# Merge gates of a two-layer hybrid block: one plain projection over 1152 tokens, or plain products for 512 and Strassen's products for 640

## Chip, cores, metric

One core of a Trainium2 chip. The metric is device time of the whole program in microseconds (us). Before the change three runs took 2002.78, 2003.73 and 2006.33 us (median 2003.73).

## What is computed

Two layers over 1152 tokens (128 context, 1024 latent) of width 1024. In each layer h is the normalised, modulated input; `h @ w_in` gives the inputs of three branches (Fourier mixing, retention, windowed attention) and, in its last 3072 columns, the merge gates. At the end of a layer:

```python
ga, gb, gc = jnp.split(jax.nn.sigmoid(mg), N_BRANCH, axis=-1)
merged = ga * (ya @ w_pa) + gb * (yb @ w_pb) + gc * (yc @ w_pc)
out = merged @ w_out
x = x + gate * rms_norm(out, g_post)
```

`mg` is 1152 x 3072 with a contraction over 1024; ya and yb have 256 columns, yc (the attention's output) has 512.

## The kernel before

Tokens lie along the free axis: `HH` and `HL` hold h transposed, as a high part (a 32-bit type that TensorE multiplies in one pass, "f32r") and the low rest, 8 blocks of 128 rows by 1152 tokens each. Every projection multiplies in three terms: high weight by high h, high weight by low h, low weight by high h. A weight unit is 1024 x 128: SP loads it to `raw` (two buffers, 512 KB), ACT casts the high part (L174), POOL subtracts the low part (L175), both with three buffers.

The gates are made in `branch` (L923), once per branch `br` and block `j` of 128 output columns. For each of three chunks of 384 tokens `proj_t` (L214) puts 24 matmuls into a PSUM bank of tag `pj` (two banks), ACT takes the tanh (L957, sigmoid as 0.5 + 0.5 tanh), PE multiplies the branch's y by its projection (L960 to L962), and DVE forms (1 + tanh) times that (L963). Branch 0 stores the sum to DRAM (`scr_m0`), branch 1 loads it, adds its own on POOL (L975) and stores (`scr_m1`), branch 2 adds the last and keeps it in the tiles `M0` to `M7`. From these comes h for the output projection (L1207, L1208).

Branches 0 and 1 stand in the program behind the attention (L983 to L1176), whose chain is QK on PE (L1057), maxima on DVE (L1071, L1075), exp on ACT (L1094), transposes on PE (L1111), casts on ACT and DVE (L1114, L1115), PV on PE (L1117, L1118). A list scheduler of the framework, with a timeline of its own, sets one fixed order for each engine's queue, and puts the branches' matmuls between those of the attention. Each engine works through its queue in order and waits on semaphores. All DMAs are issued by SP, also in order. `tick` (L481) adds a step of the next modulation vector: one load and two DVE operations on 128x256 (L446).

## Time and profile before

| | |
|---|---|
| median of three runs | 2003.73 us |
| the profiled execution | 2000.78 us, span 1999.0 us |
| PE busy | 1947.7 us (97%) |
| DVE, ACT, POOL busy | 51%, 34%, 28% |
| DMA | 230.53 MB, 115 GB/s on average |

A matmul's busy time overlaps the next one's, so a share near 100% means that PE had something in flight, and the price of a matmul is the distance from its start to the next start. The layers lie at about 100 to 960 us and 960 to 1999 us; attention with its interleaved gates at about 400 to 790 and 1390 to 1770 us; branch 2 after it.

### The profile page before, as it was taken

The numbers are of one execution on the slowest core, as the hardware profiler recorded it, in microseconds if no ns is written. First come the engines' busy times: TensorE is split into PE (matmuls) and PEld (weight loads), VectorE is DVE, ScalarE is ACT, GpSimd is POOL, SyncE is SP. The second block draws the span as 40 slices with busy tenths as digits, with TensorE's granted clock in tenths as the row PEclk, the third lists the DMA queues.
The fourth block names the chain that finished last, engine by engine and source line by source line (L and its number), as shares of the span: only waits on it lengthen the run. The fifth ranks groups of instructions, "written<-read, shape, count | busy, mean of one in ns | idle before, by whom it ended". The sixth has DMA issues, their size and how long they took to land.

```text
span 1999.0 us, 29840 instructions
## 1 busy us (share of the span) xinstructions
PE 1947.7 (97%) x11022; PEld 1790.3 (90%) x11022; DVE 1010.4 (51%) x2575; ACT 676.5 (34%) x1535; POOL 550.4 (28%) x424
## 2 busy tenths in 40 slices
PE   5999899999999999999999999999999999999998
PEld 2898788999999999999878978899999999999987
DVE  6735657556677765104675262443555665410411
ACT  2522111235555444114331212022555554421411
POOL 2222232111122332434441214122121222333442
PEclk9999999999999999999999999999999999999999
DMA  8323554353333334223344235234422433422142
GB/s 292 106 72 98 137 156 136 112 177 99 103 119 113 117 107 146 80 89 128 116 142 98 63 96 163 73 118 135 116 87 84 120 103 95 145 90 83 59 154 85
DMA packets 245186, 230.53 MB, mean 115 GB/s; under 512 B 37920, under 2 KB 215856, under 8 KB 244784
## 3 DMA queue, kind: packets, MB, share of 16 engines
q1 hardware_dynamic: 245040, 228.62, 37.8%
q8 instruction: 87, 1.43, 0.3%
q14 instruction: 59, 0.48, 0.1%
HBM read 170.14 MB, written 58.42 MB: 114 GB/s over the span
## 4 chain that ended last, share of the span: by engine, by line
PE 84%; DMA 6%; DVE 5%; issue 2%; ACT 2%; POOL 1%; SPq 1%; DVEq 0%; POOLq 0%; ACTq 0%
PE pj L218 13%; PE pj L220 13%; PE pj L219 13%; PE pj L228 5%; PE pj L229 5%; PE pj L230 5%; PE tr L1111 3%; DMA raw<-in_w_in 2%; PE sl L1057 2%; PE pv L1118 2%; PE pv L1117 2%; PE sl L962 2%; PE pj L960 2%; PE sl L960 2%; PE pj L961 2%
## 5 line engine op out<-in xcount | busy, mean ns | idle before, releaser
L218 PE MATMUL pj<-HH,uh 128*128 128x384 f32 x1440 | 491.7, 341 | 9.0 <-DVE grz L237 2.9
L219 PE MATMUL pj<-HL,uh 128*128 128x384 f32 x1440 | 486.2, 338 | 0.0
L220 PE MATMUL pj<-HH,ul 128*128 128x384 f32 x1440 | 486.0, 337 | 0.0
L175 POOL TENSOR_TENSOR ul<-raw,uh 128x1024 fp32r<-128x1024 f32 x80 | 192.2, 2403 | 481.1 <-ACT uh L174 380.4
L218 PEld LDWEIGHTS pj<-HH,uh 128*128 128x128 f32 x1440 | 271.5, 189 | 14.3 <-ACT mth L957 4.9
L219 PEld LDWEIGHTS pj<-HL,uh 128*128 128x128 f32 x1440 | 271.7, 189 | 1.6
L220 PEld LDWEIGHTS pj<-HH,ul 128*128 128x128 f32 x1440 | 271.6, 189 | 1.5
L174 ACT CAST uh<-raw 128x1024 fp32r<-128x1024 f32 x80 | 83.9, 1049 | 179.3 <-PE pj L219 124.6
L446 DVE SCALAR_TENSOR_TENSOR macc<-mw,siluc,macc 128x256 f32<-128x256 f32 x224 | 135.3, 646 | 10.9 <-DMA mw<-in_w_mod 10.9
L228 PE MATMUL pj<-uh,HH 128*128 128x512 f32 x336 | 133.5, 398 | 3.9 <-ACT kv L546 1.8
L229 PE MATMUL pj<-ul,HH 128*128 128x512 f32 x336 | 132.6, 395 | 0.0
L230 PE MATMUL pj<-uh,HL 128*128 128x512 f32 x336 | 132.5, 394 | 0.0
L963 DVE SCALAR_TENSOR_TENSOR M<-M,sl 128x384 f32<-128x384 f32 x48 | 26.6, 554 | 201.8 <-PE sl L962 196.6
L1094 ACT ACTIVATE E<-E,NM 128x640 f32<-128x640 f32 (+1 forms) x128 | 101.9, 798 | 64.1 <-DVE NM L1090 63.9
L1115 DVE TENSOR_TENSOR El<-tr,Eh 128x512 fp32r<-128x512 f32 x132 | 88.9, 685 | 46.3 <-ACT Eh L1114 46.0
L1114 ACT CAST Eh<-tr 128x512 fp32r<-128x512 f32 x132 | 74.7, 587 | 88.8 <-PE tr L1111 87.1
L975 POOL TENSOR_TENSOR mth<-mth,ml 128x384 f32<-128x384 f32 x48 | 51.4, 1071 | 178.0 <-DVE mth L963 114.3
L963 DVE SCALAR_TENSOR_TENSOR mth<-mth,pj 128x384 f32<-128x384 f32 x96 | 52.9, 551 | 62.5 <-ACT mth L957 32.0
L1111 PE MATMUL tr<-ident,E 128*128 128x128 f32 x528 | 84.0, 272 | 0.2 <-ACT E L1094 0.2
L975 POOL TENSOR_TENSOR M<-M,mrow 128x384 f32<-128x384 f32 x48 | 48.6, 1015 | 124.9 <-DVE M L963 66.5
L1075 DVE CUSTOM_DVE_ANT_0 E<-sl,mask,m 128x384 f32<-128x384 f32 (+1 forms) x128 | 72.1, 578 | 17.4 <-PE sl L1057 17.0
L228 PEld LDWEIGHTS pj<-uh,HH 128*128 128x128 f32 x336 | 63.2, 188 | 19.0 <-ACT kv L546 2.0
(316 smaller groups left out, 4038.4 us busy)
## 6 DMA issues: line engine op xcount, KB each, us to landing
raw<-in_w_in SPq DMA_DIRECT2D x84, 512.0 KB
scr_m<-mth SPq DMA_DIRECT2D x96, 192.0 KB
mw<-in_w_mod SPq DMA_DIRECT2D x128, 128.0 KB
scr_n<-ns SPq DMA_DIRECT2D x36, 256.0 KB
ml<-scr_m SPq DMA_DIRECT2D x48, 192.0 KB
mrow<-scr_m SPq DMA_DIRECT2D x16, 576.0 KB
big<-in_w_mod SPq DMA_DIRECT2D x16, 512.0 KB
raw<-in_w_out SPq DMA_DIRECT2D x16, 512.0 KB
```

The source lines that it names most:

```text
L175: POOL.tensor_tensor(out=lo, in0=raw, in1=f(hi), op=ALU.subtract)
L218: PE.matmul(acc, hi[:, k, :], HH[:, k, tok], start=(k == 0), stop=False)
L219: PE.matmul(acc, hi[:, k, :], HL[:, k, tok], start=False, stop=False)
L220: i = PE.matmul(acc, lo[:, k, :], HH[:, k, tok], start=False, stop=(k == KT - 1))
L228: PE.matmul(acc, a, hi[:, k % 2, :], start=(k == 0), stop=False)
L229: PE.matmul(acc, a, lo[:, k % 2, :], start=False, stop=False)
L230: i = PE.matmul(acc, b, hi[:, k % 2, :], start=False, stop=(k == KT - 1))
L446: DVE.scalar_tensor_tensor(out=accs[s], in0=w, scalar=siluc[:, k, s : s + 1], in1=accs[s], op0=ALU.mult, op1=ALU.add,)
L975: POOL.tensor_tensor(out=th, in0=th, in1=ml, op=ALU.add)
L1094: ACT.activation(Es[hh][:, 0:nk], srcs[hh], AF.Exp, bias=NM[t][:, hs + hh : hs + hh + 1], scale=0.125, accum_out=DEN[t][:, hs + hh : hs + ...
L1111: PE.transpose(pt[:, hh, hp_, :], Es[2 * hp_ + hh][:, n * P : (n + 1) * P], ident)
L1115: DVE.tensor_tensor(out=El, in0=pt, in1=f(Eh), op=ALU.subtract)
```

## The change

The gates of a layer are now made in two parts, after the attention in the program text and mixed into it by the scheduler.

**Front** (`gates_front`): tokens 0 to 511, all three branches, one bank of 512 columns and 24 matmuls per unit. **Back** (`gates_back`): tokens 512 to 1151, by Strassen's scheme in Winograd's form. h for these tokens is cut into four blocks (upper and lower half of the contraction, 320 tokens left and right), a pair of weight units into four blocks of 512 x 128. Seven products of 12 matmuls with 320 columns take the place of eight. Their h operands are B11, B21, B22 as they lie, and T1 to T4, differences of the blocks (`differences`), written over HH and HL where the front's tokens and block B12 were. Their weight operands are blocks and differences, formed on POOL and DVE for each pair. The products are summed partly in PSUM, partly on DVE into the tiles `th` (tag `gt`, four buffers of 128x640). The 512 weight columns of a unit are loaded and cast again for the back. Gates of branch 2 are stored to a new DRAM tensor `scr_g`. At the end `merge` loads them and the sums, multiplies only yc by its projection, and holds yc in HH and HL, so that its loads follow the last product that reads there.

Source lines of the changed file are one to three later up to the branches, and in the attention L1057 is L1207, L1071 is L1221, L1075 is L1225, L1115 is L1265.

```diff
+        def gates_front():
+
+            tk = slice(0, CT)
+            for br in range(3):
+                YH, YL = inputs_of(br, 0, CT) if br < 2 else (None, None)
+                for j in range(KT):
+                    hi, lo = unit_t(w_in, C_MG + br * D + j * P)
+                    w = weights_of(mA, br, j, 2) if br < 2 else None
+                    acc = pj([P, CT])
...
+                    th = mk(mA, [P, 2 * HN], "gt", bufs=4)[:, :CT]
+                    ACT.activation(th, acc, AF.Tanh, scale=0.5)
+                    tick()
+                    gated_sum(br, j, th, 0, CT, [tk], YH, YL, w)
...
+        def differences():
+
+            for k in range(4):
+                u, v = (mk(mA, [P, 2, HN], "gt", bufs=4) for _ in range(2))
+                b12, b11, b22, b21 = u[:, 0], u[:, 1], v[:, 0], v[:, 1]
+                for o, b in ((b12, B12), (b11, B11), (b22, B22), (b21, B21)):
+                    POOL.tensor_tensor(out=o, in0=f(part(HH, b, k)), in1=f(part(HL, b, k)), op=ALU.add)
+                DVE.tensor_tensor(out=b11, in0=b12, in1=b11, op=ALU.subtract)
+                DVE.tensor_tensor(out=b12, in0=b22, in1=b12, op=ALU.subtract)
+                DVE.tensor_tensor(out=b22, in0=b22, in1=b11, op=ALU.subtract)
+                DVE.tensor_tensor(out=b21, in0=b21, in1=b22, op=ALU.subtract)
+                for src, b in ((b22, T2), (b12, T3), (b11, T1), (b21, T4)):
...
+                    ACT.copy(h, src)
+                    DVE.tensor_tensor(out=lo, in0=src, in1=f(h), op=ALU.subtract)
...
+            o11 = operand(a11, POOL)
...
+            POOL.tensor_tensor(out=s3, in0=a11, in1=a21, op=ALU.subtract)
+            POOL.tensor_tensor(out=a21, in0=a21, in1=a22, op=ALU.add)
+            DVE.tensor_tensor(out=s2, in0=a21, in1=a11, op=ALU.subtract)
+            os2 = operand(s2, DVE)
+            DVE.tensor_tensor(out=s2, in0=a12, in1=s2, op=ALU.subtract)
+            x = pj([P, HN])
+            product(x, o11, B11, True, False)
+            ACT.copy(th[1][:, lt], x)
+            y = pj([P, HN])
+            product(y, os2, T2, True, False)
+            add(th[0][:, rt], th[1][:, lt], y)
+            product(x, operand(a12, POOL), B21, False, True)
+            tanh(0, lt, x)
+            product(y, operand(s3, POOL), T3, False, False)
+            add(th[1][:, rt], th[1][:, lt], y)
+            z = pj([P, HN])
+            product(z, operand(a21, DVE), T1, True, False)
+            add(th[1][:, rt], th[1][:, rt], z)
+            tanh(1, rt)
+            product(y, operand(a22, POOL), T4, False, True)
+            add(th[1][:, lt], th[1][:, lt], y)
+            tanh(1, lt)
+            product(z, operand(s2, POOL), B22, False, True)
+            add(th[0][:, rt], th[0][:, rt], z)
+            tanh(0, rt)
...
+        def merge(pl, M):
+
+            YH, YL = ([H[:, kt, :] for kt in range(4)] for H in (HH, HL))
+            cs = range(NCH - 1, -1, -1)
...
+                mrow = mk(pl, [P, TOK], "mrow", bufs=2)
+                SP.dma_start(mrow, ma_d[1][rows, :])
+                grow = mk(pl, [P, TOK], "grow", bufs=2)
+                SP.dma_start(grow, gc_d[rows, :])
...
-        branch(0, mA, mA, 0, None)
-        branch(1, mA, mA, 0, None)
+        gates_front()
+        gates_back()
```

`operand` casts a 128x512 block on ACT (L1026) and subtracts the rest on the engine named (L1027). `gated_sum` multiplies ya or yb by its projection (L940 to L942, six matmuls per 320 or 512 columns), forms the product on DVE (L963), adds branch 0's sum on POOL for branch 1 (L970) and stores (L971).

Three places in the queues. First DVE in layer 0's attention, between the maxima of one pair of heads (E_957, sc_959) and their masked maxima (sl_960). Before:

```order
L1071 TENSOR_SCALAR E_957_4635,m_956_4634<-sc_959_4637 128x256
L1071 TENSOR_SCALAR E_958_4636,m_956_4634<-sc_959_4637 128x256
L1115 TENSOR_TENSOR El_946_4600<-tr_944_4594,Eh_945_4599 128x512
L1075 ISA E_957_4635,m_956_4634<-sl_960_4638,mask_628_3544,m_956_4634 128x384
L1075 ISA m_956_4634 128x1
```

The same place now (gt_1539 to gt_1544 hold the blocks of h, HL is the low part):

```order
L1006 TENSOR_TENSOR gt_1541_7059<-gt_1541_7059 128x320
L1221 TENSOR_SCALAR E_957_4635,m_956_4634<-sc_959_4637 128x256
L1221 TENSOR_SCALAR E_958_4636,m_956_4634<-sc_959_4637 128x256
L1009 TENSOR_TENSOR gt_1540_7042<-gt_1540_7042 128x320
L1265 TENSOR_TENSOR El_946_4600<-tr_944_4594,Eh_945_4599 128x512
L1265 TENSOR_TENSOR El_949_4611<-tr_947_4605,Eh_948_4610 128x512
L1007 TENSOR_TENSOR gt_1541_7059<-gt_1542_7060,gt_1541_7059 128x320
L1015 TENSOR_TENSOR HL_14_78<-gt_1540_7042,HH_13_77 128x320
L1225 ISA E_957_4635,m_956_4634<-sl_960_4638,mask_628_3544,m_956_4634 128x384
```

Between two instructions of the attention stand up to three of the differences; the stretch from the first difference to the last has 70 rows, 32 of them differences.

On PE around the same attention tiles (pv_937), before, the gap is filled from a projection whose operands were ready:

```order
L219 MATMUL pj_1460_6922<-HL_14_78,uh_1450_6869 128x384
L220 MATMUL pj_1460_6922<-HH_13_77,ul_1451_6870 128x384
L960 MATMUL pj_1462_6949<-yh0_1439_6839,bh_1453_6875 128x384
L961 MATMUL pj_1462_6949<-yl0_1440_6840,bh_1453_6875 128x384
L962 MATMUL pj_1462_6949<-yh0_1439_6839,bl_1454_6876 128x384
L1057 MATMUL sl_960_4638<-K1_631_3550,Q_930_4545 128x384
L1057 MATMUL sl_960_4638<-K2_632_3551,Q_930_4545 128x384
L1117 MATMUL pv_937_4571<-Eh_939_4577,VS_742_3902 128x512
```

Now it is filled with single matmuls of the second product (pj_1554, operand T2):

```order
L1207 MATMUL sl_960_4638<-K1_631_3550,Q_930_4545 128x384
L1207 MATMUL sl_960_4638<-K2_632_3551,Q_930_4545 128x384
L1267 MATMUL pv_937_4571<-Eh_939_4577,VS_742_3902 128x512
L1035 MATMUL pj_1554_7127<-HL_14_78,uh_1549_7101 128x320
L1036 MATMUL pj_1554_7127<-HH_13_77,ul_1550_7102 128x320
L1268 MATMUL pv_937_4571<-El_940_4578,VS_742_3902 128x512
L1267 MATMUL pv_937_4571<-Eh_942_4588,VS_814_4148 128x512
```

The product's other matmuls stand singly in the following 65 rows, each behind the part of T2 that it reads.

Third, SP at the step from the gates to `merge` in layer 0 (raw: units of w_out or, in the first row below, the first weight unit of branch 2; scr_m0_1: the last two sums; M7, M6: loads of yc). Before, at the step to branch 2, the loads of yc stood right behind the attention's last store:

```order
L188 DMA raw_1704_8653<-in_w_in 128x8x128
L978 DMA scr_m0_1<-mth_1620_7996 128x384
L1158 DMA scr_y0<-Y4_1247_5634 128x4x128
L941 DMA M6_1639_8050<-scr_y0 128x384
L941 DMA M7_1641_8054<-scr_y0 128x384
```

Now:

```order
L1111 DMA M7_1861_9150<-scr_y0 128x384
L205 DMA raw_1936_9649<-in_w_out 128x2x512
L205 DMA raw_1940_9658<-in_w_out 128x2x512
L971 DMA scr_m0_1<-gt_1820_8938 128x640
L205 DMA raw_1943_9664<-in_w_out 128x2x512
L971 DMA scr_m0_1<-gt_1821_8939 128x640
L1111 DMA M6_1859_9146<-scr_y0 128x384 x6
L1120 DMA grow_1883_9308<-scr_g0 128x1152
```

Half of yc's loads (the six into M6) are issued behind the stores of the last pair's sums and behind w_out's units, which wait for a `raw` buffer.

## Rows read from the trace of the kernel before

**Rows 1.** The page, parts 1 and 2: PE's busy time, and the granted clock by slice.

```profile
PE 1947.7 (97%) x11022; PEld 1790.3 (90%) x11022; DVE 1010.4 (51%) x2575; ACT 676.5 (34%) x1535; POOL 550.4 (28%) x424
PEclk9999999999999999999999999999999999999999
```

**Rows 2.** Who waited for whom, PE from 350 to 960 us: total, times, longest us.

```profile
PE pj L218 <- ACT mth L957: 0.6, 2, 0.3
```

**Rows 3.** Timeline of PE: start us, us, line, what, width; 512 columns, six starts apart.

```profile
1300.35 0.39 PE L228 MATMUL pj<-uh,HH 128*128 128x512 f32 x1
1301.74 0.39 PE L228 MATMUL pj<-xh,HH 128*128 128x512 f32 x1
```

**Rows 4.** Timeline of PE: 384 columns, 29 starts apart.

```profile
1312.02 0.33 PE L218 MATMUL pj<-HH,uh 128*128 128x384 f32 x1
1317.05 0.34 PE L220 MATMUL pj<-HH,ul 128*128 128x384 f32 x1
```

**Rows 5.** Timeline of PE: two matmuls of 256 columns, two of 384, the next.

```profile
641.05 0.40 PE L1057 MATMUL sc<-K,Q 128*128 128x256 f32 x2
641.28 0.51 PE L1057 MATMUL sl<-K,Q 128*128 128x384 f32 x2
641.63 0.34 PE L218 MATMUL pj<-HH,uh 128*128 128x384 f32 x1
```

**Rows 6.** Single lines, DVE: duration ns min/median/max, first and last start us.

```profile
L446 DVE SCALAR_TENSOR_TENSOR macc<-mw,siluc,macc x224: 467/478/2645, 125.6 to 1195.2; 128x256 f32<-128x256 f32 x112
L1208 DVE TENSOR_TENSOR HL<-M,HH x144: 271/277/2145, 905.3 to 1900.5; 128x128 fp32r<-128x128 f32 x144
L1115 DVE TENSOR_TENSOR El<-tr,Eh x132: 670/685/693, 440.5 to 1726.4; 128x512 fp32r<-128x512 f32 x132
L963 DVE SCALAR_TENSOR_TENSOR mth<-mth,pj x96: 536/553/557, 404.3 to 1743.8; 128x384 f32<-128x384 f32 x96
```

**Rows 7.** Timeline of DVE at 725 us.

```profile
725.15 0.55 DVE L963 SCALAR_TENSOR_TENSOR mth<-mth,pj 128x384 f32<-128x384 f32 x1
725.62 2.27 DVE L446 SCALAR_TENSOR_TENSOR macc<-mw,siluc,macc 128x256 f32<-128x256 f32 x2
```

**Rows 8.** Timeline of POOL over the same moment.

```profile
724.35 2.38 POOL L175 TENSOR_TENSOR ul<-raw,uh 128x1024 fp32r<-128x1024 f32 x1 [5.56 <-PE sc L1057]
726.70 0.92 POOL L951 TENSOR_TENSOR bl<-braw,bh 128x256 fp32r<-128x256 f32 x1
```

**Rows 9.** Groups of instructions, DVE from 440 to 740 us: busy us, mean ns.

```profile
L446 DVE SCALAR_TENSOR_TENSOR macc<-mw,siluc,macc 128x256 f32<-128x256 f32 x58 | 40.2, 731 | 0.0
```

**Rows 10.** Busy by stretch: us, then PE, PEld, DVE, ACT, POOL, PEclk, DMA share, GB/s.

```profile
560.00:620.00 60.00, 60.00 (x370) 57.89 (x369) 44.21 (x115) 30.93 (x71) 14.37 (x11) 1.00 0.41 124
sum 300.00, PE 298.62 PEld 286.67 DVE 206.38 ACT 151.39 POOL 69.69; mean PE 59.72 PEld 57.33 DVE 41.28 ACT 30.28 POOL 13.94
```

**Rows 11.** Groups by form, POOL: busy us, mean ns.

```profile
L1156 POOL TENSOR_TENSOR gt<-gt,rb 128x512 f32<-128x512 f32 x18 | 23.2, 1291 | 107.2 <-DMA rb<-scr_r 47.5 <-DMA ml<-scr_m 12.7 <-PE tr L1111 12.2
L975 POOL TENSOR_TENSOR mth<-mth,ml 128x384 f32<-128x384 f32 x48 | 51.4, 1071 | 178.0 <-DVE mth L963 114.3 <-DMA ml<-scr_m 24.8 <-DVE El L1115 12.4
```

**Rows 12.** Groups by form, ACT.

```profile
L942 ACT CAST yh<-M 128x384 fp32r<-128x384 f32 x24 | 12.0, 514 | 14.1 <-DMA M<-scr_y 14.0
```

**Rows 13.** Timeline of the DMA queue on SP: a load of 256 KB.

```profile
805.36 0.37 SPq L947 DMA_DIRECT2D braw<-in_w_branch_c  x1
```

**Rows 14.** Busy by stretch of 1 us: the end of that load, then three loads together.

```profile
807.00:808.00 1.00, 1.00 (x8) 1.00 (x7) 0.56 (x1) 0.00 (x0) 1.00 (x1) 1.00 0.55 164
808.00:809.00 1.00, 1.00 (x8) 1.00 (x7) 0.00 (x0) 0.62 (x1) 0.73 (x2) 1.00 0.00 0
811.00:812.00 1.00, 1.00 (x8) 1.00 (x7) 0.56 (x1) 0.00 (x0) 0.17 (x1) 1.00 0.99 298
```

**Rows 15.** Busy by stretch of 4 us: a wait of PE, and the clock behind it.

```profile
240.00:244.00 4.00, 1.15 (x7) 0.83 (x6) 1.04 (x2) 2.22 (x4) 3.51 (x2) 1.00 0.16 48
244.00:248.00 4.00, 4.00 (x17) 4.00 (x16) 3.10 (x5) 0.00 (x0) 1.16 (x1) 0.61 0.76 189
```

More of the change, by code (lines that the diff above doesn't have):

```diff
@@ new lines, in weights_of, with mixed @@
+        def weights_of(pl, br, j, nk):
+            braw = mk(pl, [P, nk, P], "braw")
+            SP.dma_start(braw, wbs[br][:, j * P : (j + 1) * P].rearrange("(k p) f -> p k f", p=P))
+            bh = mk(pl, [P, nk, P], "bh", F32R, bufs=2)
+            bl = mk(pl, [P, nk, P], "bl", F32R, bufs=2)
+            ACT.copy(bh, braw)
+            POOL.tensor_tensor(out=bl, in0=braw, in1=f(bh), op=ALU.subtract)
+            return bh, bl
+        def mixed(pb, w, YH, YL, tok):
+            bh, bl = w
+            nk = len(YH)
+            for kt in range(nk):
+                PE.matmul(pb, bh[:, kt, :], YH[kt][:, tok], start=(kt == 0), stop=False)
+                PE.matmul(pb, bh[:, kt, :], YL[kt][:, tok], start=False, stop=False)
+                PE.matmul(pb, bl[:, kt, :], YH[kt][:, tok], start=False, stop=(kt == nk - 1))
@@ new lines, in inputs_of @@
+        def inputs_of(br, t0, n):
+            YH, YL = [], []
+            for kt in range(2):
+                yh, yl = (mk(mA, [P, 2 * HN], f"{x}{kt}", F32R)[:, :n] for x in ("yh", "yl"))
+                yr = mk(mA, [P, 2 * HN], "gt", bufs=4)[:, :n]
+                SP.dma_start(yr, y_d[br * 256 + kt * P : br * 256 + (kt + 1) * P, t0 : t0 + n])
+                ACT.copy(yh, yr)
+                DVE.tensor_tensor(out=yl, in0=yr, in1=f(yh), op=ALU.subtract)
+                YH.append(yh)
+                YL.append(yl)
+            return YH, YL
@@ new lines, in gated_sum @@
+        def gated_sum(br, j, th, t0, n, tks, YH, YL, w):
+            rows = slice(j * P, (j + 1) * P)
+            if br < 2:
+                for tk in tks:
+                    pb = pj([P, tk.stop - tk.start])
+                    mixed(pb, w, YH, YL, tk)
+                    anchor["dve"] = DVE.scalar_tensor_tensor(
+                        out=th[:, tk], in0=th[:, tk], scalar=1.0, in1=pb, op0=ALU.add, op1=ALU.mult
+                    ).ins
+                    tick()
+            if br == 1:
+                ml = mk(mA, [P, 2 * HN], "gt", bufs=4)[:, :n]
+                SP.dma_start(ml, ma_d[0][rows, t0 : t0 + n])
+                POOL.tensor_tensor(out=th, in0=th, in1=ml, op=ALU.add)
+            SP.dma_start((gc_d if br == 2 else ma_d[br])[rows, t0 : t0 + n], th)
@@ new lines, in hybrid_step, with operand @@
+        free_half = []
+        def operand(src, eng):
+            if not free_half:
+                t = [wp.tile([P, 1024], F32R, tag=x, bufs=3, name=nm(x)) for x in ("uh", "ul")]
+                for h in (1, 0):
+                    free_half.append([x[:, h * 512 : h * 512 + 512].rearrange("p (k f) -> p k f", k=4) for x in t])
+            hi, lo = free_half.pop()
+            ACT.copy(hi, src)
+            eng.tensor_tensor(out=lo, in0=src, in1=f(hi), op=ALU.subtract)
+            return hi, lo
@@ new lines, in merge @@
+                w = weights_of(pl, 2, j, 4)
+                rows = slice(j * P, (j + 1) * P)
+                mrow = mk(pl, [P, TOK], "mrow", bufs=2)
+                SP.dma_start(mrow, ma_d[1][rows, :])
+                grow = mk(pl, [P, TOK], "grow", bufs=2)
+                SP.dma_start(grow, gc_d[rows, :])
+                for c in cs:
+                    tok = slice(c * CH, (c + 1) * CH)
+                    pb = (pj if c % 2 else sl)([P, CH])
+                    mixed(pb, w, YH, YL, tok)
+                    DVE.scalar_tensor_tensor(
+                        out=M[j][:, tok], in0=grow[:, tok], scalar=1.0, in1=pb, op0=ALU.add, op1=ALU.mult
+                    )
+                    POOL.tensor_tensor(out=M[j][:, tok], in0=M[j][:, tok], in1=mrow[:, tok], op=ALU.add)
@@ L1189, in hybrid_step @@
             M.append(mk(mst.enter_context(pool("mg", side="right")), [P, TOK], f"M{j}"))
-        with pool("mg2", side="right") as m2, pool("mg3", side="right") as m3:
+        with pool("mg2", side="right") as m2:
             tick(1000)
-            branch(2, m2, m3, 0, M)
+            merge(m2, M)
         mod_bank[0] = tr
```

123 lines of the change are left out of this document (66 added, 57 removed).

## Prediction

> **What bounds the kernel.** I read the page first: PE is busy for 97% of the span, and every digit of the granted clock is a 9 [rows 1]. The next question is whether PE waits at all where the gates lie. The view of who waited for whom has 0.6 us for PE over all of 350 to 960 us [rows 2]. So every matmul removed there is time won at its start-to-start price, and every wait that is put there is time lost in full. The prices come from the timeline of PE: 0.2317 us for 512 columns (1.39 over six) [rows 3], 0.1734 for 384 (5.03 over 29) [rows 4], 0.115 for 256 (0.23 over two) [rows 5]. They lie on a line with the number of columns, so 320 columns should cost 0.144. The other engines have slack on average, not everywhere: between 440 and 740 us PE is busy for 298.62 of 300 us, DVE for 206.38, ACT for 151.39, POOL for 69.69 [rows 10].
>
> **Matmuls removed and added, per layer.** Before: 24 units of 72 matmuls with 384 columns, 1728 x 0.1734 = 299.6 us. After: 24 units of 24 matmuls with 512 columns, 576 x 0.2317 = 133.5, and 12 pairs of 7 products of 12 matmuls with 320 columns, 1008 x 0.144 = 145.2; together 278.7. The projections of ya and yb cost 288 x 0.1734 = 49.9 before, and 96 x 0.2317 + 192 x 0.144 = 49.9 after. yc's projection is the same. PE saves **20.8 us per layer, 41.6 in all**. 320 columns have no row. The nearest on both sides are 256 and 384; at their prices the 1200 matmuls would cost 35 us per layer less or more. I take the line, because three widths lie on it. That T4 is read in two pieces of 160 columns has no row either; I take it at the same price, within these bounds.
>
> **The step from front to back, in the middle of the attention.** The differences overwrite what the front's last product reads, so they stand between the two. From the end of the front to the last matmul on T2, PE's queue holds 48 matmuls with 320 columns (6.9 us), 16 with 256 (1.8), 14 with 384 (2.4), 14 with 512 (3.2), and 24 with 128, at most 0.115 each (2.8): 17.1 us. Over the same stretch DVE must do 70 instructions, 32 of them differences. In the stretch of before, a DVE instruction took 0.384 us on average (44.21 over 115) [rows 10], and the nearest row to a difference, 384 columns, is followed after 0.47 us by the next [rows 7]. At 0.384 that makes 26.9 us. DVE can begin only some 2.4 us late, since the attention's product that it needs stands 14 rows behind the front on PE.
>
> To this comes a delay that the rows show for one kind of instruction. L446 and L1208, whose inputs all lie in SBUF, take at most 2.645 and 2.145 us where the median is 0.478 and 0.277, while L1115 and L963, which read one input from PSUM, never exceed 0.693 and 0.557 over 132 and 96 instructions [rows 6]. One such case can be seen: at 725.62 us two L446 take 2.27 us together [rows 7], just as long as POOL is on its subtraction of 2.38 us, which ends when they end [rows 8]. Over 440 to 740 us L446 took 731 ns on average [rows 9] with POOL busy for 23% [rows 10]: 0.25 us too much each. The Trainium skill (SBUF — State Buffer, section "Who interferes with whom") says that a DVE instruction with two SBUF inputs and a GpSimd instruction that reads SBUF exclude each other, and that the later one is fully blocked. The trace agrees in kind: 2.645 us against at most 0.693 where one input is in PSUM. 33 of the 70 are of that kind, and POOL has some 20 us of sums there (16 of 320 columns, five of 512 at 1.291 [rows 11]), so it is busy for more than 23%; I take 0.25 us as it stands, 8 us. DVE then ends at 2.4 + 26.9 + 8 = 37.3 us, and PE is out of work after 17.1: a stall of **20 us per layer**. Bounds: 10 without any delay and with an early start (26.9 - 17.1), 25 with 0.4 us each.
>
> **The rest of the attention with Strassen's products.** PE has more than 160 us of work there, DVE about 120 plus delays on 57 more instructions with two SBUF inputs (57 x 0.25 = 14). On average that fits; I take 4 us per layer for single late sums, 0 to 10.
>
> **Pairs of branch 1.** A pair needs all four buffers `gt`: two `th`, two for branch 0's sums. The copy L1069 of the next pair writes `th`, and so waits for the store of the last one. From the end T of the seventh product: 24 matmuls of the branch's projection (3.5 us) and DVE's product, T + 4.1; POOL's addition of 640 columns, 1.5 us by 1.071 for 384 and 1.291 for 512 [rows 11], T + 5.6; the store of 320 KB, 2.9 us by the 256 KB issued at 805.36 [rows 13] whose bytes end between 807 and 808 [rows 14], T + 8.5; ACT's copy, 0.5 [rows 12], T + 9.0. PE has the projection and two products of the next pair until then, T + 6.9. The wait is 2.1 us at each of three steps; at the first one SP has the load of `mrow` in front of the second store, and it waits for the first store's end, which makes it 5. **9 us per layer** (3 to 15).
>
> **The step to merge.** Before, yc's loads stood behind the attention's last store and were ready long before use. Now the six into M6 stand on SP behind both stores of the last pair. POOL has an addition (T + 3.9), then the low part of a unit of w_out, 2.38 us [rows 8] (T + 6.3), then the second addition (T + 7.9); the load into M6 is issued at T + 8.3, lands at T + 10.4, is cast by T + 11. PE needs it at T + 3.5. **8 us per layer** (2 to 10).
>
> **The clock behind these waits.** Where PE was busy for 1.15 of 4 us, the granted clock of the next 4 us was 0.61, on the way to the lower of its two levels, 1.2 GHz [rows 15]: about 4 x 0.39 = 1.6 us lost. 2 us per layer for the waits together (0 to 4).
>
> **What costs nothing, and its cover.** The weights of the back are loaded twice (12.6 MB per layer), and gc goes out and in. In `merge` 1.41 MB come per block of 36 matmuls of 384 columns (6.24 us), 226 GB/s; the rows show 298 GB/s where loads run together [rows 14], and two buffers hide the rest. If that cover failed, `merge` would pay it eight times. ACT has half of its time free [rows 10].
>
> **Sum.** 20 + 4 + 9 + 8 + 2 = 43 us per layer against 20.8 saved. From the profiled execution, 2000.8 us (2.95 below the median of the three runs): 2000.8 - 41.6 + 86 = **2045 us**. With all low bounds (15 per layer) 1989, with all high ones (64) 2087.
>
> **Rivals.**
> *DVE keeps up, and the saving arrives.* This ends on the other side. What decides is whether the last low part of T2 is written within 17.1 us of the front's last matmul. If DVE forms its first differences while the front still multiplies, and its rows go at the distance of the attention's own and without delay, PE never runs dry; with the pairs and `merge` at their low ends or better (2 to 3 us per layer) the time is 2000.8 - 41.6 + 2 x 3 = 1965 us. For it: only part of the 70 rows stands ahead of T2's last part on DVE, and DVE is free for a third of the stretch before [rows 10]. Against it: single matmuls of T2 stand between attention rows as if each had to be waited for.
>
> *DVE and POOL exclude each other everywhere.* Then each pair of the back pays for its four DVE instructions with two SBUF inputs ahead of a product, at about 0.65 us (what two L446 lost [rows 7], halved): 2.6 us per pair, 31 per layer where I took 4. 2045 + 2 x 27 = 2099 us. For it: the long L446. Against it: at PE the delay counts only where the sum is already late, and before it never reached PE [rows 2]. The page of the Trainium skill named above would have it so: its lock holds for the whole instruction; 2099 is what the sum would be by it.
>
> *Narrow matmuls don't pay by their columns.* Should 320 columns cost what 384 do, for loading weights or for the split operand, the saving turns into a loss of 14 us per layer: 2045 + 70 = 2115. Against it: 256 columns at 0.115 [rows 5].
>
> **How the numbers follow.** About 0.2%, 4 us, is what a measurement of this kernel can tell from no change. My forecast, stalls of 15 to 64 us per layer, has 0.65; of that 0.06 lies within 4 us of 2000.8 and 0.04 below. DVE keeping up has 0.24, exclusion 0.08, narrow matmuls 0.03. Faster: 0.24 + 0.04 = 0.28; same: 0.06; slower: 0.55 + 0.08 + 0.03 = 0.66. The forecast's own range is 1989 to 2087. Cases of both signs hold the chance, so the range reaches down to the first rival, with its own spread of 2 us: 1963 to 2087. The two costly rivals stay outside.
>
> **What would show it.** Right: PE at 12 matmuls of 320 columns in about 1.73 us; in each layer's attention one stretch of 20 us in which PE waits for DVE's low parts of T2; waits of 2 to 5 us for L1069 in branch 1; a wait of about 8 us at `merge` for casts of M6; DVE differences longer than 0.5 us on average while POOL sums. Wrong: PE busy through the differences; a different distance of the 320 column matmuls; waits in all 12 pairs alike; or waits for DMA in every block of `merge`.

## The result, and the profile after

The changed kernel takes 2094.8 us (median of four runs, 2094.41 to 2098.39), the kernel before, on the same chips, 2005.03 (2002.78 to 2006.91): a ratio of 1.0452, with a 95% interval of 1.0434 to 1.047. It is slower, by more than the forecast of 2045 us and by more than the upper end of its range, 2087. The profiled execution took 2098.39 us, its span is 2096.6.

The page, parts 1 and 2, of the changed kernel (PE's and POOL's totals, granted clock by slice), beside [rows 1]:

```profile
PE 1957.5 (93%) x10734; PEld 1714.5 (82%) x10734; DVE 1235.0 (59%) x2847; ACT 796.6 (38%) x1783; POOL 844.1 (40%) x640
PEclk8999999999998999989999999999999899998999
```

PE has fewer instructions (10734, before 11022), POOL is busy for 844 us (before 550), and the clock is no longer granted in full in every slice; its mean is 0.972 against 0.998.

The price of 320 columns, from the timeline of PE: eleven starts lie between these two rows, 1.61 us or 0.1464 each.

```profile
614.82 0.31 PE L1034 MATMUL pj<-HH,uh 128*128 128x320 f32 x1
616.43 0.31 PE L1036 MATMUL pj<-HH,ul 128*128 128x320 f32 x1
```

So narrow matmuls pay by their columns. With 0.1465 in place of 0.144 the 1200 of them cost 3 us more per layer, and the saving is 17.8 us per layer instead of 20.8. What came on top must be waits. The largest on PE's side (who waited for whom: total, times, longest us):

```profile
PE sl L940 <- ACT HH L1112: 18.0, 2, 9.3
PE pj L940 <- DVE gt L963: 11.4, 10, 4.1
PE pj L940 <- DVE gt L1054: 9.1, 6, 2.8
PE pv L1268 <- DVE El L1265: 6.6, 9, 1.6
PE pj L1034 <- DVE gt L1054: 6.2, 8, 1.6
PE pj L1034 <- ACT HH L1014: 4.5, 5, 1.2
```

The first is merge's wait for yc's casts, once per layer. The others are the projections (L940), the attention's PV (L1268) and the products (L1034), which wait for DVE's sums (L1054), for its gated products (L963), for its low parts (L1265), or for the cast of a difference (L1014).

To compare runs I went through PE's timeline from start to start, took off each instruction's price (0.112 us for 128 columns, 0.116 for 256, 0.1465, 0.1734 and 0.2317 for 320, 384 and 512) and summed what is left. This is **PE's loss**: waits, the restart behind them, and matmuls at the lower of the two clock levels (1.2 in place of 2.4 GHz, 0.5 in the granted clock). The stages are: front; step (the 36 us behind the front's last matmul); rest (to the attention's last matmul); branch 1 (to the last product); merge. Before, PE lost 6.9 and 5.3 us over the same work in the two layers. In the changed kernel:

| PE's loss, us, layer 0 / layer 1 | front | step | rest | branch 1 | merge | sum |
|---|---|---|---|---|---|---|
| changed kernel, 2094.8 us | 9.3 / 2.6 | 16.5 / 16.7 | 15.9 / 12.0 | 8.6 / 11.8 | 16.6 / 18.6 | 66.9 / 61.7 |

This closes the account. The span grew by 97.6 us; 128.6 of loss, less the 12.2 before, less 2 x 17.8 saved, make 80.8. The other 16 or 17 lie outside the gates, most of them (some 11) between the end of layer 0's merge and the front of layer 1, where the program is the same but has more short waits and 5 us of matmuls at the lower clock.

Three stretches show how the losses look. First the step. Rows of PE, DVE and POOL from their timelines (start us, us, engine, line, what, [idle before and who ended it]):

```profile
624.77 1.94 POOL L1005 TENSOR_TENSOR gt<-HH,HL 128x320 f32<-128x320 f32 x2
625.22 1.84 DVE L1015 TENSOR_TENSOR HL<-gt,HH 128x320 fp32r<-128x320 f32 x2
627.38 0.68 DVE L1265 TENSOR_TENSOR El<-tr,Eh 128x512 fp32r<-128x512 f32 x1
628.12 0.50 PE L1268 MATMUL pv<-El,VS 128*128 128x512 f32 x1 [1.52 <-DVE El L1265]
```

Two low parts of a difference take 1.84 us together, as long as POOL is on two of its sums (624.77 to 626.71). The attention's low part El stands behind them in DVE's queue, and PE waits 1.52 us for it. Busy time by stretch (us, then PE, PEld, DVE, ACT, POOL, granted clock, DMA share, GB/s), the step in the first row, the start of merge in the second:

```profile
611.00:647.00 36.00, 27.50 (x125) 21.80 (x124) 35.01 (x86) 21.06 (x50) 19.55 (x18) 0.81 0.23 68
905.00:950.00 45.00, 35.67 (x192) 34.69 (x191) 13.32 (x27) 7.46 (x17) 23.77 (x22) 0.85 0.59 190
```

DVE is busy for 35.0 of the 36 us at the step. In both stretches the granted clock is well below 1.

Second, a place in the rest of the attention in layer 0 (same columns):

```profile
656.40 1.68 POOL L1306 TENSOR_TENSOR gt<-gt,rb 128x512 f32<-128x512 f32 x1 [1.35 <-DMA rb<-scr_r]
657.25 2.54 DVE L448 SCALAR_TENSOR_TENSOR macc<-mw,siluc,macc 128x256 f32<-128x256 f32 x2
658.04 1.47 POOL L1027 TENSOR_TENSOR ul<-sa,uh 128x512 fp32r<-128x512 f32 x1
661.13 0.68 DVE L1265 TENSOR_TENSOR El<-tr,Eh 128x512 fp32r<-128x512 f32 x1
661.86 0.50 PE L1268 MATMUL pv<-El,VS 128*128 128x512 f32 x1 [1.96 <-DMA mw<-in_w_mod]
```

Two of tick's operations take 2.54 us together while POOL is on two instructions that read SBUF; El stands four places behind them on DVE, and PE waits 1.96 us for it. The view puts this wait down to the load of `mw`, tick's weights.

Third, the end of layer 0's gates, from POOL's, DVE's, PE's, SP's and ACT's timelines:

```profile
901.04 2.38 POOL L177 TENSOR_TENSOR w0l<-raw,w0h 128x1024 fp32r<-128x1024 f32 x1 [3.46 <-ACT w0h L176]
901.77 2.06 DVE L1113 TENSOR_TENSOR HL<-M,HH 128x384 fp32r<-128x384 f32 x1 [1.28 <-ACT HH L1112]
904.29 0.41 PE L940 MATMUL pj<-yh,bh 128*128 128x320 f32 x1 [2.12 <-DVE gt L963]
904.37 1.56 POOL L970 TENSOR_TENSOR gt<-gt,gt 128x640 f32<-128x640 f32 x1 [0.94 <-POOL w0l L177]
909.74 0.34 SPq L971 DMA_DIRECT2D scr_m<-gt  x1
910.17 6.45 SPq L1111 DMA_DIRECT2D M<-scr_y  x6
914.16 1.53 ACT L1112 CAST HH<-M 128x384 fp32r<-128x384 f32 x3 [10.71 <-DMA M<-scr_y]
914.72 0.69 PE L940 MATMUL sl<-HH,bh 128*128 128x384 f32 x1 [9.29 <-ACT HH L1112]
```

L1113, the low part of a yc tile for merge, stands on DVE ahead of the gates' product L963. It waits 1.28 us for its cast, POOL's low part of w_out then holds it until that ends (2.06 us), and PE waits 2.12 us for L963. POOL's first sum follows that product, its second one more low part of w_out (905.88 to 908.23). The second store goes out at 909.74, and only then does SP issue yc's loads into M6. PE starts merge after another 9.29 us.

### The profile page after: what moved, and what is told of

Same layout as the page of the kernel before. It is cut to its first block, busy times and chain, and to the rows that moved or that the text cites. A ratio compares the mean times of both kernels' runs of the same rounds, so it can differ in the third digit from the quotient of the medians.

```text
span 2096.6 us, 30401 instructions
## 1 busy us (share of the span) xinstructions
PE 1957.5 (93%) x10734; PEld 1714.5 (82%) x10734; DVE 1235.0 (59%) x2847; ACT 796.6 (38%) x1783; POOL 844.1 (40%) x640
## 5 line engine op out<-in xcount | busy, mean ns | idle before, releaser
L1034 PE MATMUL pj<-HH,uh 128*128 128x320 f32 x672 | 217.3, 323 | 12.8 <-DVE gt L1054 6.2
L1035 PE MATMUL pj<-HL,uh 128*128 128x320 f32 x672 | 211.3, 314 | 2.8 <-DVE HL L1015 2.8
L1036 PE MATMUL pj<-HH,ul 128*128 128x320 f32 x672 | 210.5, 313 | 0.0
L983 PE MATMUL pj<-HH,uh 128*128 128x512 f32 x384 | 153.6, 400 | 3.3 <-ACT gt L988 2.9
L985 PE MATMUL pj<-HH,ul 128*128 128x512 f32 x384 | 151.9, 396 | 0.0
L984 PE MATMUL pj<-HL,uh 128*128 128x512 f32 x384 | 151.1, 394 | 0.0
L1034 PEld LDWEIGHTS pj<-HH,uh 128*128 128x128 f32 x672 | 128.9, 192 | 20.8 <-DVE gt L1054 9.3
L448 DVE SCALAR_TENSOR_TENSOR macc<-mw,siluc,macc 128x256 f32<-128x256 f32 x224 | 134.9, 647 | 11.5 <-DMA mw<-in_w_mod 11.4
L1036 PEld LDWEIGHTS pj<-HH,ul 128*128 128x128 f32 x672 | 128.5, 191 | 0.5
L1027 POOL TENSOR_TENSOR ul<-raw,uh 128x512 fp32r<-128x512 f32 x72 | 98.5, 1371 | 67.6 <-ACT uh L1026 57.3
L1265 DVE TENSOR_TENSOR El<-tr,Eh 128x512 fp32r<-128x512 f32 x132 | 89.2, 684 | 33.9 <-ACT Eh L1264 33.6
L220 PE MATMUL pj<-HH,uh 128*128 128x384 f32 x288 | 99.3, 345 | 5.9 <-DVE XL L655 2.6
L222 PE MATMUL pj<-HH,ul 128*128 128x384 f32 x288 | 98.8, 343 | 0.0
L221 PE MATMUL pj<-HL,uh 128*128 128x384 f32 x288 | 98.0, 340 | 0.0
```

Source lines behind the costliest of these rows:

```text
L448: DVE.scalar_tensor_tensor(out=accs[s], in0=w, scalar=siluc[:, k, s : s + 1], in1=accs[s], op0=ALU.mult, op1=ALU.add,)
L983: PE.matmul(acc, hi[:, k, :], HH[:, k, tk], start=(k == 0), stop=False)
L984: PE.matmul(acc, hi[:, k, :], HL[:, k, tk], start=False, stop=False)
L985: i = PE.matmul(acc, lo[:, k, :], HH[:, k, tk], start=False, stop=(k == KT - 1))
L1034: PE.matmul(acc, hi[:, k, :], part(HH, b, k), start=start and k == 0, stop=False, **kw)
L1035: PE.matmul(acc, hi[:, k, :], part(HL, b, k), start=False, stop=False, **kw)
```

## Experiments

Each ran once, beside one run of the kernel before (2003.3 for the first four, 2004.8 for the next three, 2005.3 for the next three, 1991.8 for the last). PE's loss in all of them, in us, layer 0 / layer 1; in runs with yc's own tiles the first matmuls of merge already lie among those of branch 1:

| run | us | front | step | rest | branch 1 | merge |
|---|---|---|---|---|---|---|
| changed kernel | 2094.8 | 9.3 / 2.6 | 16.5 / 16.7 | 15.9 / 12.0 | 8.6 / 11.8 | 16.6 / 18.6 |
| e1, no differences of h | 2066.2 | 8.4 / 4.1 | 1.4 / 1.3 | 10.5 / 17.2 | 11.3 / 9.5 | 17.0 / 19.3 |
| e2, POOL writes only | 2060.2 | 7.6 / 3.9 | 15.6 / 16.9 | 1.8 / 3.6 | 4.3 / 5.8 | 17.9 / 18.0 |
| e3, yc's own tiles | 2059.1 | 9.8 / 4.1 | 16.6 / 16.3 | 15.6 / 7.2 | 8.1 / 8.7 | 3.0 / 5.3 |
| e4, plain back | 2037.8 | 9.0 / 4.5 | 2.1 / 0 | 0.3 / 0.5 | 6.2 / 6.2 | 0.2 / 0.9 |
| e5, POOL writes as long | 2058.1 | 8.4 / 2.7 | 16.0 / 16.0 | 0 / 1.0 | 5.1 / 5.2 | 18.0 / 17.9 |
| e11, the same, with load waits | 2066.0 | 9.0 / 3.8 | 15.9 / 15.1 | 4.4 / 0.9 | 7.3 / 8.1 | 17.1 / 17.9 |
| e6, e3 and weights on one engine | 2047.7 | 7.8 / 3.6 | 18.0 / 17.4 | 8.2 / 2.2 | 10.3 / 9.3 | 5.8 / 6.5 |
| e7, e3 and T3 first | 2085.3 | 14.8 / 3.5 | 16.3 / 14.1 | 22.8 / 13.9 | 9.4 / 11.5 | 3.0 / 8.0 |
| e8, e6 and step's sums write only | 2047.5 | 7.0 / 3.9 | 14.9 / 13.1 | 12.8 / 3.6 | 9.7 / 9.1 | 5.3 / 5.4 |
| e9, e1, e3 and e5 at once | 1999.0 | 7.4 / 2.2 | 0 / 0 | 1.1 / 0.5 | 3.7 / 5.6 | 5.4 / 6.4 |
| e10, e6 and no differences | 2021.7 | 7.9 / 4.2 | 4.4 / 0 | 9.6 / 5.1 | 6.9 / 9.4 | 7.4 / 6.9 |

### The step: the differences left out (e1)

```diff
-            differences()
```

> The differences of h (their sums on POOL, their casts on ACT, 32 subtractions on DVE per layer) are left out; the products read what lies where T1 to T4 would be. Theory 1, the step from front to back is lost to DVE's differences: the 16.5 and 16.8 us that PE loses around 615 and 1635 us go, the other losses of the back stay, and the time is 2095 - 33 = about 2060. Rival, the step is late because of the weight operands of the first pair and not of T: PE waits there all the same for low parts of the weights, and the time stays above 2085.

Measured: 2066.2 us, and the step's loss is 1.4 and 1.3 us. The differences are the cause, and the first pair's weights are not late. Of the 30.5 us that vanish at the step 29 arrive in the time, though the losses of the other stages moved by up to 5 us each.

### The pairs among the attention: what POOL reads (e2, e5, e11)

```diff
-            eng.tensor_tensor(out=lo, in0=src, in1=f(hi), op=ALU.subtract)
+            if eng is POOL:
+                POOL.memset(f(lo), 0.0)
+            else:
+                eng.tensor_tensor(out=lo, in0=src, in1=f(hi), op=ALU.subtract)
...
-            POOL.tensor_tensor(out=s3, in0=a11, in1=a21, op=ALU.subtract)
-            POOL.tensor_tensor(out=a21, in0=a21, in1=a22, op=ALU.add)
+            POOL.memset(s3, 0.0)
+            POOL.memset(a21, 0.0)
```

> In the pairs of the back, every POOL instruction on weights (five low parts, two sums per pair) is replaced by a memset of the same tile, which reads nothing; DVE keeps all its instructions. Theory 2, DVE's instructions with two SBUF inputs are held up by POOL's reads and this is what PE waits for in the pairs: L1064 falls from 1.66 to about 0.69 us and L1066 from 1.27 to 0.69, PE loses at most 8 us per layer in the eight pairs in the attention (19 now) and the time is about 2095 - 2 x 18 = 2060. Rival, DVE's queue is late by the amount of its work and the two banks of PSUM turn over too soon: DVE's instructions become short, PE still loses 15 us and more in these pairs, and the time is above 2080.

Measured: 2060.2 us, with 1.8 and 3.6 us lost in the rest, as theory 2 has it. But a memset took only 0.527 us where the sums took 1.3, and did not wait for ACT's casts, so POOL was also earlier. The next run gives POOL back its length and its place behind ACT's casts.

```diff
-                POOL.memset(f(lo), 0.0)
+                ACT.copy(lo[:, 0, 0:1], src[:, 0, 0:1])
+                blank(f(lo))
...
+        def blank(t):
+            POOL.memset(t, 0.0)
+            POOL.memset(t, 0.0)
+            POOL.memset(t[:, 0:2], 0.0)
```

> As in the run with POOL's memsets, but each of the seven POOL instructions of a pair becomes two memsets of the whole tile and one of its half (0.527 us were measured for one, so about 1.3 us together, as long as before), behind a one-column copy on ACT that stands where POOL waited for ACT's cast: POOL is as busy and as late as in the changed kernel, and reads nothing. Theory 2a, it is POOL's reads that hold up DVE: L1064 stays at 0.7 us, PE loses at most 5 us per layer between the step and the end of the attention (15.9 and 12.0 in the changed kernel), and the time is 2055 to 2070. Rival 2b, it is POOL's lateness (DVE's L1064 waited 9.7 us in layer 0 for POOL's L1063): PE loses 10 us and more there, and the time is above 2075.

Measured: 2058.1 us, and nothing and 1.0 us lost in the rest. Groups by form of DVE, 650 us to the end of the pairs, first in the changed kernel (us busy, mean ns, idle before and who ended it), then in e5, where L1064 is L1073 and L1066 is L1075:

```profile
L1064 DVE TENSOR_TENSOR sb<-raw 128x512 f32<-128x512 f32 x11 | 18.3, 1660 | 14.2 <-POOL raw L1063 9.7 <-POOL ul L1027 4.4
L1066 DVE TENSOR_TENSOR sb<-raw,sb 128x512 f32<-128x512 f32 x11 | 13.9, 1268 | 0.1
L448 DVE SCALAR_TENSOR_TENSOR macc<-mw,siluc,macc 128x256 f32<-128x256 f32 x13 | 9.8, 780 | 0.0
```

```profile
L1075 DVE TENSOR_TENSOR sb<-raw,sb 128x512 f32<-128x512 f32 x11 | 7.6, 692 | 0.8 <-DMA raw<-in_w_in 0.6
L1073 DVE TENSOR_TENSOR sb<-raw 128x512 f32<-128x512 f32 x10 | 6.9, 690 | 3.6 <-POOL raw L1037 2.2 <-issue 1.3
L448 DVE SCALAR_TENSOR_TENSOR macc<-mw,siluc,macc 128x256 f32<-128x256 f32 x12 | 5.3, 483 | 0.0
```

With POOL as long on each tile, but only writing, L1064 goes from 1.66 to 0.69 us, L1066 from 1.27 to 0.69, L448 from 0.78 to 0.48. The Trainium skill (SBUF — State Buffer, section "Who interferes with whom") says just this: a DVE instruction with two SBUF inputs contends with a GpSimd instruction that reads SBUF, not with one that only writes it. The 1.66 and 0.69 us agree.

One thing was still mixed in: DVE's wait for POOL's sums, at the head of its queue, fell from 14.2 to 3.6 us, since a memset needs no load. The last run puts the wait for both units' loads back.

```diff
+            ACT.copy(s3[:, 0, 0:1], a21[:, 0, 0:1])
             blank(s3)
+            ACT.copy(a21[:, 0, 0:1], a22[:, 0, 0:1])
             blank(a21)
```

> The run with POOL's memsets of the same length, with one thing put back: two one-column copies on ACT make POOL wait for both units' loads before the two sums of a pair, as it did in the changed kernel (POOL waited 12.5 us for a load before L1063 between 650 and 850 us, and DVE's L1064 9.7 us behind it). Theory 2a, POOL's reads alone: PE loses at most 5 us per layer between the step and the end of the attention, as in the run before (nothing and 1.0), and the time stays within 4 us of 2058. Rival 2c, a good part was DVE's L1064 waiting at the head of its queue for POOL's late sums: DVE waits for POOL's sums 9 us and more again, PE loses 6 us or more per layer there, and the time is above 2066.

Measured: 2066.0 us, where 2062 was the most that theory 2a allowed. On its chip the kernel before took only 1991.8, but outside the gates e11's trace is about as long as e5's (some 960 us), so the two can be set side by side. DVE waits again ahead of that instruction (8.3 us, against 3.6 in e5 and 14.2 in the changed kernel), mostly for POOL's sums, and the instruction stays short (groups by form, 650 to 880 us; L1075 is the changed kernel's L1064):

```profile
L1075 DVE TENSOR_TENSOR sb<-raw 128x512 f32<-128x512 f32 x11 | 7.6, 692 | 8.3 <-POOL raw L1037 5.9 <-ACT ul L1028 1.2 <-POOL bl L933 0.7
```

By the place, PE lost 4.4 and 0.9 us in the rest. So of the 14.0 us that the changed kernel lost there per layer on average, up to 11 go with POOL's reads, and at least 2 with the sums that start late (2.7 us lost on average here, 0.5 in e5); the lateness is only partly put back. The time was nearer to rival 2c, the place to theory 2a: branch 1 lost 2 to 3 us more than in e5.

### Merge: yc in tiles of its own (e3)

```diff
-                    n = c * 4 + kt
-                    yr = M[6 + n % 2][:, n // 2 % NCH * CH : n // 2 % NCH * CH + CH]
+                    yr = mk(pl, [P, CH], "yr", bufs=6)
```

> merge's twelve loads of yc go into six tiles of their own and no longer into M6 and M7; nothing else is changed. Theory 3, the wait at merge comes from the place of the loads behind the last stores: the waits of 9.3 us (layer 0) and 14 us (layer 1) at L940 fall under 3 us each, with the clock behind them, and the time is about 2095 - 22 = 2073. Rival, the low part of the weights, or mrow and grow, come just as late: the wait stays above 6 us per layer under another name, and the time above 2083.

Measured: 2059.1 us, 36 less. Waits of PE from 880 to 960 us in that run:

```profile
PE pv L232 <- DVE HL L1355: 2.1, 1, 2.1
PE sl L940 <- ACT HH L1111: 1.4, 1, 1.4
PE pj L940 <- DVE gt L1054: 1.2, 1, 1.2
PE sl L941 <- DVE HL L1112: 0.5, 1, 0.5
```

Of the 9.3 us 1.4 are left: six loads now go out in branch 1, and merge begins while the last pair is still under way. More came back than the wait, since PE's idle time in the last projection went too: 13.6 and 13.3 us at merge. (For layer 1 the expectation had 14 us at L940; the wait alone was 8.7, and 14.3 with the two waits of the last projection.) The other 9 of the 36 came back elsewhere, most of them in layer 1's rest and branch 1, and their cause was not looked for.

### Strassen's products taken back (e4)

```diff
-                for jp in range(4):
-                    th = gate_pair(C_MG + br * D + jp * 256)
...
+                for j in range(KT):
+                    hi, lo = unit_t(w_in, C_MG + br * D + j * P)
...
+                    for h, o in ((lt, CT), (rt, CT + HN)):
+                        acc = pj([P, HN])
+                        for k in range(KT):
+                            tk = slice(o, o + HN)
+                            PE.matmul(acc, hi[:, k, :], HH[:, k, tk], start=(k == 0), stop=False)
```

> The back's 640 tokens get plain products again (24 matmuls for each 320 tokens and block), with no differences of h or of weights; front, stores and merge as in the changed kernel. If Strassen's scheme with its sums is what PE waits for in the attention and in branch 1, only the waits of the front (5 us more than before per layer) and of merge (15) stay, and the narrower matmuls (1344 per layer, 0.0025 us above the line): 2001 + 2 x 23 = about 2048, with under 5 us lost by PE between the front and branch 1's end. If the two parts as such (buffers gt, stores, loading weights twice) are the cause, PE loses 15 us and more there, and the time is above 2075.

Measured: 2037.8 us. Step and rest lose 2.1 us at most, as expected, so the loss there belongs to Strassen's scheme (its sums, differences and short products) and not to the two parts. Branch 1 still loses 6.2 us with plain products. Merge loses under 1 us, which was not foreseen and makes the run faster than expected, by 10 us in all. The two parts alone are no gain: without Strassen's scheme the kernel is 34 us slower than the one before on the same chip, most of it by the front, branch 1, the narrower matmuls and the stretches outside the gates. The timeline of SP in e4 shows that six of yc's loads go out already behind the attention:

```profile
811.23 2.69 SPq L1119 DMA_DIRECT2D M<-scr_y  x6
```

Probably M6 lies where the changed kernel has the tiles of the weights' sums (`sa`, `sb`), which the plain back lacks; that was not tried by itself.

### The weights on one engine (e6)

```diff
-            POOL.tensor_tensor(out=s3, in0=a11, in1=a21, op=ALU.subtract)
-            POOL.tensor_tensor(out=a21, in0=a21, in1=a22, op=ALU.add)
-            DVE.tensor_tensor(out=s2, in0=a21, in1=a11, op=ALU.subtract)
-            os2 = operand(s2, DVE)
+            W.tensor_tensor(out=s3, in0=a11, in1=a21, op=ALU.subtract)
+            W.tensor_tensor(out=a21, in0=a21, in1=a22, op=ALU.add)
+            W.tensor_tensor(out=s2, in0=a21, in1=a11, op=ALU.subtract)
+            os2 = operand(s2, W)
...
+                    th = gate_pair(C_MG + br * D + jp * 256, DVE if br == 1 else POOL)
```

> On top of the kernel with yc's own tiles (2059): in the pairs of branches 2 and 0, among the attention, POOL forms all eleven... that is all nine sums and low parts of the weights; in branch 1, behind the attention, DVE forms them all. By theory 2a the four DVE instructions per pair that POOL held up are gone from the attention's DVE queue, and in branch 1 POOL reads half as long: PE loses at most 5 us per layer in the rest of the attention (15.6 and 7.2) and 5 in branch 1 (8.1 and 8.7), about 2059 - 19 = 2040. Rival: POOL, with 9 x 1.3 = 11.7 us per pair and one chain of five before the second product, becomes late itself, PE waits for its low parts, and the time stays above 2052.

(A pair has eleven such instructions, seven low parts and four sums; "nine" is a slip.) Measured: 2047.7 us. The rest falls to 8.2 and 2.2 us; branch 1 does not fall. In layer 0 one wait of 5.5 us for a copy L1069 makes about half of branch 1's 10.3. The time lies between the two expectations, nearer to the rival's 2052 than to 2040; but from the step to the end of layer 0's branch 1 no wait of PE is named for POOL's low parts, as the rival would have it.

### Less work at the step (e7, e8, e10)

```diff
+                if br == 2:
+                    difference_t3()
...
-                DVE.tensor_tensor(out=b11, in0=b12, in1=b11, op=ALU.subtract)
-                DVE.tensor_tensor(out=b12, in0=b22, in1=b12, op=ALU.subtract)
-                DVE.tensor_tensor(out=b22, in0=b22, in1=b11, op=ALU.subtract)
-                DVE.tensor_tensor(out=b21, in0=b21, in1=b22, op=ALU.subtract)
+                DVE.tensor_tensor(out=b11, in0=t3, in1=b11, op=ALU.add)
+                split(b11, T2, k)
+                DVE.tensor_tensor(out=b22, in0=b22, in1=b11, op=ALU.subtract)
+                DVE.tensor_tensor(out=b21, in0=b21, in1=b11, op=ALU.subtract)
```

> On top of the kernel with yc's own tiles (2059): T3 is formed during the front (it needs none of the front's tokens), and after the front T2 = T3 + B11, T1 = B22 - T2, T4 = B21 - T2, so that 24 instead of 32 of DVE's instructions stand between front and back, and T2's last part behind about 20 instead of 28. Theory 1, DVE's queue sets the step: PE's loss there falls from 16.6 and 16.3 to about 11 per layer, and the time is about 2048. Rival, POOL's sixteen sums, which stay, set it: the loss stays above 14 per layer and the time above 2054.

Measured: 2085.3 us, a miss: the step still loses 16.3 and 14.1 us, and front and rest lose more than in e3. These are the numbers of the rival, that POOL's sums set the step. But between 620 and 656 us DVE is still busy for 33.0 of 36 us (34.8 in e3), so it hardly stood idle for POOL's sums. The 24 differences left there take 16.9 us, the 32 of e3 18.8: they got longer, 0.70 us on average against 0.59. What made them longer, and front and rest worse, was not settled.

```diff
-                    POOL.tensor_tensor(out=o, in0=f(part(HH, b, k)), in1=f(part(HL, b, k)), op=ALU.add)
+                    for _ in range(3):
+                        POOL.memset(o, 0.0)
```

> On top of the run with the weights on one engine (2048): the sixteen sums of the blocks of h that POOL forms at the step (about 0.95 us each) become three memsets of the same tile (about as long together), which read nothing; h's differences are therefore wrong values, with all instructions of DVE and ACT in place. Theory 1, the step is lost to the amount of DVE's work (DVE busy for 35.0 of the 36 us from 611 us in the changed kernel), of which POOL's reads make up some 5 us (L1015 0.65 us on average against 0.48): PE's loss at the step falls from 18.0 and 17.4 to 12 or 13, and the time is about 2038. Rival, the delays are most of it: the loss falls under 8 per layer and the time under 2030.

Measured: the step loses 14.9 and 13.1 us (e6: 18.0 and 17.4), about what theory 1 had: POOL's reads make some 4 us of the step's loss per layer. DVE's busy time in the same 36 us falls from 34.39 in e6 to this row's 31.20:

```profile
611.00:647.00 36.00, 28.27 (x146) 23.83 (x145) 31.20 (x86) 23.81 (x58) 19.11 (x46) 0.81 0.25 70
```

The time did not follow (2047.5), since the rest lost 12.8 us in layer 0 instead of 8.2.

The third run of this kind is e6 without the call of `differences`.

> The run with the weights on one engine (2048), without the differences of h. By theory 1 the step's 18.0 and 17.4 us go and nothing else: about 2048 - 33 = 2015, with 8 and 2 us in the rest of the attention and 10 and 9 in branch 1 as they were. Rival, the pairs behind the step then wait for POOL's eleven instructions instead: above 2025.

Measured: 2021.7 us; the step's loss falls to 4.4 and 0, and 26 us arrive, between the expected 33 and the rival's 23. With e1 it shows the same thing on two kernels.

### All three at once (e9)

The edits of e1, e3 and e5 together.

> The changed kernel with all three taken away at once: no differences of h, POOL's instructions on the weights as memsets of the same length, yc in tiles of its own. If the saving of PE's work is real (18 us per layer at the measured 0.1465 us for 320 columns) and these three are the whole loss, PE loses some 17 us per layer (8 and 4 in the front, 5 in branch 1, 3 to 5 in merge), and the time is 1990 to 2000, below the kernel before. Rival, one wait hides another behind it, or the narrow matmuls give nothing: above 2010.

Measured: 1999.0 us, with 17.6 and 14.7 us lost. So the saving of PE's work is there, and the three causes make 96 of the 128.6 us lost: without them the kernel is 6 us faster than the one before on the same chip. This run leaves out the differences and what POOL forms of the weights, so it is no kernel, but it shows about what this plan has to give: even with all three cured some 32 us of loss stay in the gates, against 12 before, and the 16 outside them stay too, which eats nearly all of the 36 saved. Of the versions that leave nothing out none beat the kernel before; the plain back (e4) takes 2037.8 us, and the fastest with Strassen's products is e6, 2047.7.

## Why the prediction was wrong, point by point

The direction was right. Two terms were mis-sized beyond their own bounds, one (branch 1) had its size by another cause than the forecast's, and one cost was not looked for. Per layer, forecast against PE's mean loss:

- **Matmuls saved**: 20.8, measured 17.8. The line between 256 and 384 columns was good to 0.0025 us, which 1200 matmuls made 3 us. A matmul on T4's two pieces of 160 columns cost as much as one of 320 in one piece, 0.147 us.
- **The front**: 0, measured 6.0: in layer 0 mostly waits of units for their tanh (L988, 5.1 of 9.3 us), in layer 1 one wait for the retention's L882. PE lost as much before over all stages (6.1), so the two cancel in the sum.
- **The step from front to back**: 20, measured 16.6. The count held: DVE's 70 instructions filled its queue (35.0 of 36 us), and e1 shows that the differences are the cause. The delays by POOL were some 4 us of it (e8), where I had 8. It was not one stretch of waiting for T2's low parts, as I had it: only 2.8 us, in layer 1, are named for these (L1015). PE worked on in between, and its named waits, 8.3 and 8.6 us, are mostly for casts of differences and for steps of the attention behind them; the rest is restarts and about 4.5 us of matmuls at the lower clock.
- **The rest of the attention**: 4 with bounds 0 to 10, measured 14.0. **This is the step that failed.** I compared sums over the stretch ("On average that fits") although I had the delays in hand. An average hides that what PE needs next from DVE stands in a queue: each product of 1.76 us needs its bank of PSUM back from DVE within about the next product, and the attention's steps stand in the same queue, so a DVE instruction that is held for a microsecond can become a wait of PE. PE's named waits in the rest are 8.1 and 7.3 us: 2.7 and 2.8 for sums and gated products (L1054, L963), 3.4 and 4.5 for the attention's steps on DVE (L1221, L1225, L1265), and the 2.0 shown above. e5 shows that POOL's reads are the cause, e11 that they are up to 11 of the 14 us.
- **Pairs of branch 1**: 9, measured 10.2. The size was right by luck, the mechanism was not. I had PE wait for L1069 at each of three steps, 2 to 5 us each. PE waits for it once, in layer 1 (who waited for whom, 1844 to 1916 us); in layer 0 DVE's sums waited 5.5 us for L1069, but no wait of PE is named for it:

```profile
PE pj L940 <- DVE gt L1054: 4.1, 2, 2.8
PE pj L1034 <- ACT gt L1069: 1.6, 1, 1.6
PE pj L940 <- DVE gt L963: 1.1, 2, 0.6
PE pj L1034 <- DVE gt L1054: 0.6, 1, 0.6
```

  The other named waits are for DVE's sums and gated products. e5 takes away half of the loss, and plain products (e4) still lose 6.2; what makes the remaining half is open.
- **The step to merge**: 8 with bounds 2 to 10, measured 17.6. The order of things was as forecast (stores, then loads into M6, then casts; e3 shows it), but it began late: the last projection took 8 us instead of 3.5, because merge's own low parts (L1113) stood ahead of the gates' sums and products on DVE, waited there for their casts and were held by POOL's low part of w_out. The loads went out at 910.17 us, 12.9 after the seventh product's end instead of 8.3, and took 4.0 us to the cast instead of 2.1. This term's bound was made from one undisturbed chain. (A block of merge loads 1.44 MB, not 1.41; in the blocks behind merge's first no wait of PE is named, so that cover held.)
- **The clock**: 2 (0 to 4). Matmuls that started in stretches of 0.5 of the clock (1.2 GHz) cost 8.5 and 8.9 us more in the gates, contained in the losses above, and 5 us more outside them. The row that I took it from [rows 15] was one wait, while here many short waits lie close together; the rows of 611 and 905 us show 0.81 and 0.85.
- **Outside the gates**: 0, measured 8. I had not looked for it, and its cause is open.

By these: 10.0 + 9.6 + 8 + 3 more, 3.4 less at the step, 1.2 more in branch 1, 2 less since the clock is counted within: 26 us per layer, which is the 53 us between 2045 and the profiled execution.

The **rival** that has DVE and POOL exclude each other everywhere gave 2099 us and named the mechanism that decided. Its price was not right in the place: it had 31 us per layer over all twelve pairs where the eight among the attention lost 14, and the rest of its sum was covered by merge, the stretches outside the gates and the price of 320 columns, so the agreement of 2099 with 2095 is partly luck. I gave it 0.08 because the delays had never reached PE in the kernel before [rows 2]. That was no evidence: before, 24 matmuls of 384 columns, 4.2 us, went into one bank before the other one was wanted again, so a delay of a microsecond in DVE's turn on that bank could not reach PE; no run tried this by itself. The rival that DVE keeps up, and the one on narrow matmuls, are refuted by e1 and by the price of 320 columns.

## What to carry to other kernels

When a change splits long PE products into short ones with sums between them, don't ask whether DVE's busy share fits: ask how long DVE may be late before PE misses a PSUM bank or another result from DVE's queue, and compare that with the longest, not the mean, duration of what stands in its queue. Count which DVE instructions take both inputs from SBUF and when POOL reads; giving one kind of work to one engine (e6) was worth 11 us more than sharing it between the two. And where a scratch region is shared to save space, look at what else its reuse is tied to: own tiles for twelve loads were worth 27 us here at merge, 36 in the time.
